# Scores of two key heads alternated in halves of the TensorE rows, with a new order of the attention steps

## The chip, the cores and the metric

The kernel runs on one core of one Trainium2 chip. The metric is the device time of one execution in microseconds (us). Engines are PE (TensorE, matrix products), DVE (VectorE), ACT (ScalarE), POOL (GpSimd) and SP (SyncE, which issues the transfers).

## What is computed

One inference step of a hybrid backbone of two layers, on 640 tokens of width 1024: 128 context tokens and 512 latent ones. A layer is an FFN, a mixer and a second FFN, each behind a modulated norm. The mixer has four parts of width 256, and this text is about three of them:

```python
IN_SPLITS = (H_A * HEAD_DIM, KV_A * HEAD_DIM, KV_A * HEAD_DIM, ...)     # H = 4 heads, KV = 2 key heads, HEAD_DIM = 64
def dense_attention(q, k, v, sink):                                      # B, and A's context tokens
    ...
    s = jnp.einsum('bqkgd,bskd->bkgqs', qi, k).astype(jnp.float32) * scale
    p = attn_probs(s, sink).astype(v.dtype)
    return jnp.einsum('bkgqs,bskd->bqkgd', p, v)
def window_attention(q, k, v, kc, vc, sink):                             # A: keys of +-128 tokens and 256 cached ones
    ...
    p = attn_probs(jnp.concatenate([s_ctx, s_band], axis=-1), sink).astype(v.dtype)
def retention_scan(q, k, v, log_g, S0):                                  # D, both directions
    ...
    inner = jnp.einsum('bhqd,bhsd->bhqs', qi, ki) * decay_mask
```

A is attention 0 (windowed, with a sink logit in the softmax), B attention 1 (dense). Both have four query heads in two groups g of two, one for each of the two key heads kv. The queries and keys are normed by head, scaled by a gain and turned by a rotary table. Part C is a recurrent branch.

## The kernel before, in words

Operands are float32, and a product is made of three products of their high and low parts, hi by hi, hi by lo, lo by hi (`mm3`, lines 271 to 275). ACT makes the high part of a weight (L168, whi or wp) and DVE the low part (L169, wlo).

Attention is worked in 20 items for each of A and B: five blocks b of 128 query tokens (the context, then four latent ones), two groups g, two key heads kv. A head has 64 channels, so the operands of the scores fill 64 of PE's 128 rows: kv 0 the upper half, kv 1 the lower. An item runs as follows. `scores`: PE makes the scores in a tile of two PSUM banks (sc): three products for the 256 cached keys, three for the tokens' own keys; in A one or two products with a mask (L1257) follow, on all 128 rows. DVE takes the maximum (mx, L1264) and its negative multiple (nm, L1268 or L1270); ACT takes the exponential of the scores and its sum (P, L1273), in A that of the sink (esink, L1276); DVE adds (L1277), inverts (rc, L1279) and scales (P, L1280). `trans`: PE transposes P in tiles of 128 columns (pt, L1290) and ACT copies (PT, L1291). `pv`, for both kv together: PE multiplies with the values (ao, L1299), ACT and DVE make the two parts (mxh, L1303; mxl, L1304).

The other work of the same stretch: `qkv`, the projections of queries, keys and values (nat, L1025 to L1027), with ACT's copies and squares (q, qsq), DVE's sum (qss, L1178, L1179), POOL's inverse root (qrr, L1181), DVE's product (q, L1183), POOL's gain (q, L1185), DVE's sine part (r, L1197), POOL's cosine part (q, L1200), DVE's addition (q, L1201); then transposes (tr, L1159) into the parts qkh and qkl (L1160, L1161). And `down`: output products of parts C and D (dn, twelve a call here), which DVE adds to the residual (x, L682).

`retention` makes scores in `scores` (rs, L1063, through `mm3`): for each of four key chunks j and two calls c, three products of 512 columns for one head, then three for the other.

What sets the order: the steps are Python generators, and the string ORDER has one letter for each step taken: m and M are scores and the rest of attention 0, n and N those of attention 1, p and q the two `qkv`, t and u their transposes, c the output products. "|" sets PSUM to two tiles of two banks (name S: the scores) and four of one bank (name M: nat, tr, pt, ao, dn). A scheduler with its own model then orders the instructions of each engine; each engine executes its own queue.

## Time and profile before

| | us |
|---|---|
| three runs | 2519.9, 2520.45, 2527.45 |
| median | 2520.45 |
| span of the profiled execution | 2521.9 |

The profile is of one execution, so rows are read against 2521.9 and compared with the median. Busy shares are of the whole span; the change touches the mixers only, and of these the retention (near 595 us in layer 0) and the attention (about 657 to 808 us in layer 0, 1896 to 2047 us in layer 1). A row of the timeline gives start, duration, engine, line, tiles written and read, and in brackets the time that the engine was idle before it and what ended that.

### The profile page before, as it was taken

To read this page: it belongs to the slowest core of one execution; us is meant where nothing else is said; L and a number is where in the kernel's file an instruction comes from. 1 tells how busy PE (TensorE), PEld (TensorE's weight loads), DVE (VectorE), ACT (ScalarE), POOL (GpSimd) and SP (SyncE) were. 2 spreads that over 40 slices of the span, in tenths; PEclk is the share of its full clock that TensorE was granted. 3 is DMA by queue.
4 is the path that set the end of the run, shared out by engine and by line. 5 is a ranking of instruction groups with operands and counts; after the bars stand their busy time and mean duration, and the time that the engine had idled before them with its cause. 6 is when DMAs were issued, how large, how long until landed. Compare 5 with 4: busy or idle time off the path is not lost.

```text
span 2521.9 us, 43865 instructions
## 1 busy us (share of the span) xinstructions
PE 2467.4 (98%) x17376; PEld 2365.6 (94%) x17376; DVE 1974.8 (78%) x3850; ACT 1141.8 (45%) x2271; POOL 244.8 (10%) x251
## 2 busy tenths in 40 slices
PE   7999999999999999999999999999999999999999
PEld 6999999996888999999999999999878789999999
DVE  6899989856666898988989898897656668666765
ACT  5344334563345633443463344344634556433433
POOL 2100000022420200000020000000433102000000
PEclk9999999999999999999999999999999999999999
DMA  7544344222102244443424444342110022222222
GB/s 253 185 152 138 127 129 148 94 78 67 37 18 66 93 144 134 143 133 118 141 89 148 134 142 133 119 134 78 58 60 26 18 76 76 77 67 81 87 81 71
DMA packets 92303, 261.88 MB, mean 104 GB/s; under 512 B 10049, under 2 KB 20929, under 8 KB 92097
## 3 DMA queue, kind: packets, MB, share of 16 engines
q1 hardware_dynamic: 92096, 259.07, 31.7%
q8 instruction: 137, 2.24, 0.4%
q14 instruction: 70, 0.57, 0.1%
HBM read 255.63 MB, written 3.41 MB: 103 GB/s over the span
## 4 chain that ended last, share of the span: by engine, by line
PE 67%; DVE 4%; ACT 2%; POOL 1%; issue 1%; DVEq 0%; POOLq 0%; ACTq 0%
PE dn L273 8%; PE dn L274 7%; PE dn L275 7%; PE x L274 5%; PE x L275 5%; PE x L273 5%; PE y L274 3%; PE y L275 3%; PE y L273 3%; PE pt L1290 2%; PE ao L1299 2%; PE g L274 2%; PE g L273 2%; PE g L275 1%; PE z L273 1%; PE z L274 1%
## 5 line engine op out<-in xcount | busy, mean ns | idle before, releaser
L273 PE MATMUL dn<-hidh,wp 128*128 128x320 f32 x1408 | 434.5, 311 | 0.0
L275 PE MATMUL dn<-hidh,wp 128*128 128x320 f32 x1408 | 433.9, 309 | 0.0
L274 PE MATMUL dn<-hidl,wp 128*128 128x320 f32 x1408 | 433.7, 309 | 0.2 <-DVE hidl L281 0.2
L168 ACT ACTIVATE wp<-ws 128x512 fp32r<-128x512 f32 x288 | 180.8, 630 | 393.2 <-DVE ws L215 149.9
L168 ACT ACTIVATE wp<-raw 128x512 fp32r<-128x512 f32 (+1 forms) x408 | 243.7, 611 | 212.1 <-DVE wp L169 84.2
L682 DVE SCALAR_TENSOR_TENSOR x<-dn,mod,x 128x128 f32<-128x128 f32 (+3 forms) x488 | 233.8, 518 | 126.4 <-PE dn L275 125.3
L318 DVE SCALAR_TENSOR_TENSOR junk<-wm,cond 128x1024 bf16<-128x1024 f32 x256 | 304.5, 1218 | 4.6 <-DMA wm<-in_wmod 4.5
L169 DVE TENSOR_TENSOR wp<-raw,wp 128x512 fp32r<-128x512 f32 (+1 forms) x408 | 266.2, 667 | 51.9 <-ACT wp L168 47.0
L273 PEld LDWEIGHTS dn<-hidh,wp 128*128 128x128 f32 x1408 | 264.5, 188 | 4.8 <-ACT hidh L280 3.7
L274 PEld LDWEIGHTS dn<-hidl,wp 128*128 128x128 f32 x1408 | 264.8, 188 | 0.6 <-DVE hidl L281 0.6
L275 PEld LDWEIGHTS dn<-hidh,wp 128*128 128x128 f32 x1408 | 264.6, 188 | 0.0
L169 DVE TENSOR_TENSOR wp<-ws,wp 128x512 fp32r<-128x512 f32 x288 | 197.4, 691 | 17.6 <-ACT wp L168 17.0
L274 PE MATMUL g<-hl,whi 128*128 128x320 f32 x608 | 192.6, 318 | 3.2 <-DVE hl L528 1.7
L275 PE MATMUL g<-hh,wlo 128*128 128x320 f32 x608 | 190.5, 314 | 0.0
L273 PE MATMUL g<-hh,whi 128*128 128x320 f32 x608 | 185.5, 318 | 4.5 <-ACT hh L527 2.2
L273 PE MATMUL x<-hh,wp 128*128 128x320 f32 x576 | 178.3, 310 | 1.0 <-DVE sl L613 1.0
L274 PE MATMUL x<-hl,wp 128*128 128x320 f32 x576 | 178.5, 310 | 0.0
L275 PE MATMUL x<-hh,wp 128*128 128x320 f32 x576 | 178.3, 309 | 0.0
L169 DVE TENSOR_TENSOR wlo<-raw,whi 128x1024 fp32r<-128x1024 f32 x88 | 109.8, 1249 | 61.2 <-ACT whi L168 46.0
L425 POOL TENSOR_TENSOR nrs<-nrm,neghalf 80x4 f32<-80x4 f32 x12 | 13.3, 1106 | 1377.1 <-DVE nrm L423 1377.1
L168 ACT ACTIVATE whi<-raw 128x1024 fp32r<-128x1024 f32 x88 | 92.5, 1052 | 80.5 <-PE dk L274 20.7
L274 PEld LDWEIGHTS g<-hl,whi 128*128 128x128 f32 x608 | 117.1, 193 | 5.9 <-DVE hl L454 3.5
(331 smaller groups left out, 6655.2 us busy)
## 6 DMA issues: line engine op xcount, KB each, us to landing
raw<-in_wgu SPq DMA_DIRECT2D x176, 512.0 KB, 3.5
wm<-in_wmod SPq DMA_DIRECT2D x128, 512.0 KB, 4.0
raw<-in_wd SPq DMA_DIRECT2D x64, 512.0 KB, 3.8
raw<-in_wd SPq DMA_DIRECT2D x32, 384.0 KB, 3.4
raw<-in_wint SPq DMA_DIRECT2D x20, 512.0 KB, 3.5
wm<-in_wm SPq DMA_DIRECT2D x32, 256.0 KB, 5.5
raw<-in_wqkv SPq DMA_DIRECT2D x16, 512.0 KB, 3.5
raw<-in_wocd SPq DMA_DIRECT2D x8, 512.0 KB, 3.4
```

Source lines behind the costliest of these rows:

```text
L168: S.activation(hi, src, AF.Copy)
L169: V.tensor_sub(lo, src, hi.bitcast(F32))
L273: PE.matmul(out, wh, xh, start=first, stop=False, skip_group_check=more)
L274: PE.matmul(out, wh, xl, start=False, stop=False, skip_group_check=more)
L275: mark["pe"] = PE.matmul(out, wl, xh, start=False, stop=last, skip_group_check=more)
L318: V.scalar_tensor_tensor(junk, modraw["w"], 1.0, cond[c], OP.mult, OP.mult, accum_out=modraw[(l, g)][:, c, k:k + 1])
L425: G.tensor_tensor(r, s, neghalf[:80, :4], op=OP.pow)
L682: V.scalar_tensor_tensor(x[d][:, s0:s1], pv[:, s0 - base:s1 - base], gate[:, c, d:d + 1], x[d][:, s0:s1], OP.mult, OP.add)
L1290: PE.transpose(p[:, c0 - a0:c0 - a0 + 128], P[:, c0:c0 + 128], idn)
L1299: PE.matmul(o[kv * 64:kv * 64 + 64, :128], vs[i][:, kv * 64:kv * 64 + 64], pts[kv][:, i * 128:i * 128 + 128], start=i == 0, stop=i == nb - 1)
```

## The change

`mm3s` issues the three products of two halves in turn: first product of A, first of B, second of A, and so on. The retention's scores use it. The items of an attention are now pairs (b, g): one step takes both S tiles, issues the scores of both key heads in turn, masks after them, and makes both softmaxes; one step of the rest transposes both and makes the products with v of the pair before. So m and n have 10 letters each in ORDER, and M and N 11, where they had 20 and 21. The part of ORDER from "|" on is new; the products are the same in number. Lines move by some: mx is L1268 after, nm L1271 or L1273, the exponential L1276, pt L1293, ao L1302, x L690.

```diff
+ROWS = (slice(0, 64), slice(64, 128))
 ORDER = (
-    "CaCCCCvLvrLarvvvLLLbsLvpLrprbrssrqsrsrLsptrsLpppqLp|!sputpLsptcqpcmccpMmqMmmcqtMmMmmqmMMmmqMqMcmcqMm"
-    "MuqmmqqccMMMmmmucMmMnnnuNcNNnnNnMNnnMNNmMncNncnnNNcnnNnNmnNNNMnNnNNnMccnMNNN",) * L
+    "CaCCCCvLvrLarvvvLLLbsLvpLrprbrssrqsrsrLsptrsLpppqLp|!sputpLsptcqpcmcmcpMtmqMmqMmqcMumqqMmqMmuqMmqMmq"
+    "cMuMncMnNncNncNncNncNncNncNnNncNcNcN",) * L
...
+        def mm3s(outs, whs, wls, xhs, xls, last=True):
+            n = range(len(outs))
+            for ws, xs, f, e in ((whs, xhs, True, False), (whs, xls, False, False), (wls, xhs, False, last)):
+                for i in n:
+                    PE.matmul(outs[i], ws[i], xs[i], start=f, stop=e)
...
                 def scores(j):
                     p = psS("rs")
-                    for hh in range(2):
-                        r0 = slice(hh * 64, hh * 64 + 64)
-                        ks = slice(128 + j * 128, 256 + j * 128)
-                        mm3(p[:, hh * 512:hh * 512 + 512], kh[r0, ks], kl[r0, ks], qh[r0, 128:640], ql[r0, 128:640],
-                            True, True)
+                    ks = slice(128 + j * 128, 256 + j * 128)
+                    mm3s([p[:, :512], p[:, 512:]], *([t[r, c] for r in ROWS] for t, c in (
+                        (kh, ks), (kl, ks), (qh, slice(128, 640)), (ql, slice(128, 640)))))
...
-                items = []
-                for b in range(5):
-                    for g in range(2):
-                        for kv in range(2):
-                            items.append((b, g, kv))
-                def scores(b, g, kv):
-                    p = psS("sc")
...
-                        mm3(p[:, 256:512], qh, ql, ckh[r, m * 256:m * 256 + 256], ckl[r, m * 256:m * 256 + 256], True, True)
-                        mm3(p[:, 512:512 + w], qh, ql, qkh[2][r, k0:k0 + w], qkl[2][r, k0:k0 + w], True, not band)
-                        for e, (j, i) in enumerate(band):
+                items = [(b, g) for b in range(5) for g in range(2)]
+                def scores(b, g):
+                    ps = [psS("sc") for _ in ROWS]
...
+                        mm3s([p[:, 256:512] for p in ps], *qs, *keys(ckh, ckl, slice(m * 256, m * 256 + 256)))
+                        mm3s([p[:, 512:512 + w] for p in ps], *qs, *keys(qkh[2], qkl[2], slice(k0, k0 + w)), not band)
+                        for p in ps:
+                            for e, (j, i) in enumerate(band):
...
+                    return [softmax(p[:, lo:hi], hi - lo, l * 4 + g * 2 + kv) for kv, p in enumerate(ps)], hi - lo, vs
...
-                    for b, g, kv in items:
-                        P, w, vs = q.pop(0)
-                        pts[kv] = trans(P, w)
+                    for b, g in items:
+                        Ps, w, vs = q.pop(0)
+                        pts = [trans(P, w) for P in Ps]
                         if ready:
                             pv(*ready)
-                        if kv == 1:
-                            ready = (b, g, (pts[0], pts[1]), vs)
-                            pts = {}
+                        ready = (b, g, pts, vs)
```

What the engines' queues look like at three places of layer 0 (numbers behind a name are those of the tile). PE at the start of the attention, before:

```order
L275 MATMUL dn_7147<-mxh_6985,wlo_6843 128x320
L273 MATMUL sc_7166<-qkh_6288,qkh_6286 128x128
L274 MATMUL sc_7166<-qkl_6291,qkh_6286 128x128
L275 MATMUL sc_7166<-qkh_6288,qkl_6289 128x128
L273 MATMUL dn_7183<-mxh_6567,whi_6842 128x320
```

One item, and behind it two calls of twelve dn and 24 of nat. PE after, first the pair and then what follows its twelve dn:

```order
L283 MATMUL sc_7166<-qkh_6288,qkh_6286 128x128
L283 MATMUL sc_7167<-qkh_6288,qkh_6286 128x128
L283 MATMUL sc_7166<-qkl_6291,qkh_6286 128x128
L283 MATMUL sc_7167<-qkl_6291,qkh_6286 128x128
L283 MATMUL sc_7166<-qkh_6288,qkl_6289 128x128
L283 MATMUL sc_7167<-qkh_6288,qkl_6289 128x128
L274 MATMUL dn_7200<-mxh_6567,whi_6842 128x320
```

```order
L276 MATMUL dn_7200<-mxh_6985,wlo_6843 128x320
L283 MATMUL sc_7214<-qkh_6288,qkh_6287 128x128
L283 MATMUL sc_7214<-qkl_6291,qkh_6287 128x128
L283 MATMUL sc_7214<-qkh_6288,qkl_6290 128x128
L274 MATMUL dn_7248<-mxh_6567,whi_6842 128x320
```

The first half of the second pair (sc_7214, in the place of sc_7166) now stands twelve dn behind the first pair. DVE at the same place, before:

```order
L1197 TENSOR_TENSOR r_7142<-q_7132,rsin_1362 128x8x16 x2
L1264 TENSOR_REDUCE mx_7170<-sc_7166 128x1
L1268 TENSOR_SCALAR nm_7172<-mx_7170,negsink_1376 128x1
L1201 TENSOR_TENSOR q_7132<-q_7132,r_7142 128x256
L1277 TENSOR_TENSOR sum_7175<-sum_7175,esink_7177 128x1
```

and after:

```order
L1200 TENSOR_TENSOR r_7142<-q_7132,rsin_1362 128x8x16 x2
L1268 TENSOR_REDUCE mx_7174<-sc_7166 128x1
L1268 TENSOR_REDUCE mx_7187<-sc_7167 128x1
L1204 TENSOR_TENSOR q_7132<-q_7132,r_7142 128x256
L1271 TENSOR_SCALAR nm_7176<-mx_7174,negsink_1376 128x1
L1271 TENSOR_SCALAR nm_7189<-mx_7187,negsink_1376 128x1
```

The two maxima stand together, and the addition of q stands ahead of nm, where it stood behind it. The second place is PE at the seventh windowed pair, before (scores of one item, transposes of q, then a projection):

```order
L273 MATMUL sc_7900<-qkh_6288,qkh_6286 128x384
L274 MATMUL sc_7900<-qkl_6291,qkh_6286 128x384
L1159 MATMUL tr_7852<-idn_96,q_7090 128x128
L1159 MATMUL tr_7852<-idn_96,q_7300 128x128
L1159 MATMUL tr_7852<-idn_96,q_7400 128x128
L1159 MATMUL tr_7852<-idn_96,q_7532 128x128
L1025 MATMUL nat_7859<-whi_7046,hh_5335 128x256
```

and after:

```order
L1259 MATMUL sc_7908<-masks_1364,idb_1366 128x128
L1162 MATMUL tr_7951<-idn_96,q_7748 128x128
L1162 MATMUL tr_7955<-idn_96,q_7748 128x128
L283 MATMUL sc_8033<-ckh_6854,qkh_6286 128x256
L283 MATMUL sc_8033<-ckl_6855,qkh_6286 128x256
L283 MATMUL sc_8033<-ckh_6854,qkl_6289 128x256
```

with DVE beside it:

```order
L1186 TENSOR_TENSOR q_7859<-q_7859,qrr_7865 128x256
L1200 TENSOR_TENSOR r_7869<-q_7859,rsin_1362 128x8x16 x2
L1204 TENSOR_TENSOR q_7859<-q_7859,r_7869 128x256
L1307 TENSOR_TENSOR mxl_7163<-ao_7894,mxh_7162 128x128
L1268 TENSOR_REDUCE mx_7925<-sc_7907 128x1
L1268 TENSOR_REDUCE mx_7938<-sc_7908 128x1
L1271 TENSOR_SCALAR nm_7927<-mx_7925,negsink_1376 128x1
```

Two transposes stand between the masks of a pair and the scores of the next (sc_8033, in the place of sc_7907), and the maxima of the pair before stand behind the rotary chain of q. The third place is ACT in the dense part, before:

```order
L1273 ACTIVATE P_8751,sum_8752<-sc_8740,nm_8749 128x768
L1291 ACTIVATE PT_8757<-pt_8758 128x384
L1291 ACTIVATE PT_8757<-pt_8763 128x384
L1303 ACTIVATE mxh_8265<-ao_8768 128x128
L1273 ACTIVATE P_8794,sum_8795<-sc_8783,nm_8792 128x768
L1291 ACTIVATE PT_8800<-pt_8801 128x384
```

and after:

```order
L1276 ACTIVATE P_8667,sum_8668<-sc_8649,nm_8665 128x768
L1276 ACTIVATE P_8677,sum_8678<-sc_8650,nm_8675 128x768
L1294 ACTIVATE PT_8697<-pt_8698 128x384
L1294 ACTIVATE PT_8697<-pt_8703 128x384
L1294 ACTIVATE PT_8708<-pt_8709 128x384
L1294 ACTIVATE PT_8708<-pt_8714 128x384
```

Exponentials and copies now come as two and four.

## Rows read from the trace of the kernel before

**Rows 1.** The page: busy time of each engine, and the chain that ended last.
```profile
PE 2467.4 (98%) x17376; PEld 2365.6 (94%) x17376; DVE 1974.8 (78%) x3850; ACT 1141.8 (45%) x2271; POOL 244.8 (10%) x251
...
PE 67%; DVE 4%; ACT 2%; POOL 1%; issue 1%; DVEq 0%; POOLq 0%; ACTq 0%
```
**Rows 2.** Stretches of 20 us: length, busy us by engine, granted clock, DMA share, GB/s.
```profile
720.00:740.00 20.00, 17.24 (x122) 14.41 (x120) 12.56 (x36) 8.06 (x22) 5.63 (x5) 0.83 0.04 16
...
760.00:780.00 20.00, 20.00 (x166) 16.43 (x162) 13.83 (x33) 11.12 (x27) 0.00 (x0) 1.00 0.08 27
```
**Rows 3.** Waits of PE, 640 to 820: total us, times, longest; two largest of five.
```profile
PE ao L1299 <- DVE x L682: 2.5, 1, 2.5
PE pt L1290 <- DVE P L1280: 1.7, 2, 1.5
```
**Rows 4.** Stretches of 2 us, columns as in Rows 2.
```profile
668.00:670.00 2.00, 0.55 (x7) 0.46 (x7) 1.93 (x7) 0.80 (x4) 0.72 (x1) 1.00 0.00 0
...
672.00:674.00 2.00, 2.00 (x11) 2.00 (x10) 1.65 (x11) 1.59 (x4) 0.46 (x1) 0.50 0.00 0
```
**Rows 5.** Instructions on the tile of the scores: busy us by engine (first PE).
```profile
640.00:820.00 180.00, 45.11 (x240) 28.77 (x216) 29.55 (x40) 32.74 (x80) 0.97 0.12 38
```
**Rows 6.** Timeline of PE in the dense part: start, us, engine, line, tiles.
```profile
765.06 0.38 PE L273 MATMUL sc<-ckh,qkh 64*128 64x256 f32 x1
...
766.31 0.42 PE L273 MATMUL dn<-mxh,whi 128*128 128x320 f32 x1
...
768.26 0.38 PE L273 MATMUL sc<-ckh,qkh 64*128 64x256 f32 x1
...
768.72 0.39 PE L273 MATMUL sc<-qkh 64*128 64x512 f32 x1
...
769.96 0.87 PE L1290 MATMUL pt<-idn,P 128*128 128x128 f32 x6
770.76 0.66 PE L1299 MATMUL ao<-PT,cv 128*64 128x128 f32 x8
...
772.22 0.55 PE L1290 MATMUL pt<-idn,P 128*128 128x128 f32 x3
772.70 0.38 PE L273 MATMUL sc<-ckh,qkh 64*128 64x256 f32 x1
```
**Rows 7.** Timeline of PE, then of DVE, at the first scores.
```profile
656.84 0.33 PE L273 MATMUL sc<-qkh 64*128 64x128 f32 x1
...
657.32 0.41 PE L273 MATMUL dn<-mxh,whi 128*128 128x320 f32 x1
...
661.65 0.28 DVE L1264 TENSOR_REDUCE mx<-sc 128x1 f32<-128x128 f32 x1
...
662.65 0.43 DVE L1201 TENSOR_TENSOR q<-q,r 128x256 f32<-128x256 f32 x1 [0.46 <-POOL q L1200]
```
**Rows 8.** Timeline of PE at the scores of the retention.
```profile
595.92 0.51 PE L273 MATMUL rs<-dqh,dkh 64*128 64x512 f32 x2
...
596.81 1.08 PE L1073 MATMUL ro<-pm,dvn 128*64 128x512 f32 x4
```
**Rows 9.** Timeline of DVE, then of ACT, after the two items of Rows 6.
```profile
769.61 1.82 DVE L1264 TENSOR_REDUCE mx<-sc 128x1 f32<-128x768 f32 x2
...
772.48 0.89 ACT L1273 ACTIVATE P<-sc,nm 128x768 f32<-128x768 f32 x1
...
773.35 0.86 ACT L1291 ACTIVATE PT<-pt 128x384 f32<-128x384 f32 x2
```
**Rows 10.** The chain that ended last, 705 to 730: start, us, what.
```profile
711.24 0.82 DVE mx L1264
712.06 0.33 DVE qss L1178
...
716.68 0.43 DVE q L1201
```
**Rows 11.** Groups of instructions by shape, 640 to 820: busy us, mean ns.
```profile
L1273 ACT ACTIVATE P<-sc,nm 128x640 f32<-128x640 f32 x8 | 6.4, 796 | 4.9 <-DVE nm L1268 2.6 <-DVE qss L1179 1.5 <-DVE rc L1279 0.8
```

More of the change, by code (lines that the diff above doesn't have):

```diff
@@ L1084, in retention @@
                 p = psS("rsc")
-                for hh in range(2):
-                    r0 = slice(hh * 64, hh * 64 + 64)
-                    mm3(p[:, hh * 512:hh * 512 + 128], kh[r0, 0:128], kl[r0, 0:128], qh[r0, 0:128], ql[r0, 0:128],
-                        True, True)
+                mm3s([p[:, :128], p[:, 512:640]], *([t[r, :128] for r in ROWS] for t in (kh, kl, qh, ql)))
                 pmc = thin("pmc", 256)
@@ L1231, in attention @@
                         mixed[2 * m + g] = (slot("mxh", F32R, T), slot("mxl", F32R, T))
-                items = []
-                for b in range(5):
-                    for g in range(2):
-                        for kv in range(2):
-                            items.append((b, g, kv))
-                def scores(b, g, kv):
-                    r = slice(kv * 64, kv * 64 + 64)
-                    qh, ql = qkh[g][r, b * 128:b * 128 + 128], qkl[g][r, b * 128:b * 128 + 128]
-                    p = psS("sc")
+                items = [(b, g) for b in range(5) for g in range(2)]
+                def scores(b, g):
+                    t0 = b * 128
+                    qs = [[t[r, t0:t0 + 128] for r in ROWS] for t in (qkh[g], qkl[g])]
+                    keys = lambda th, tl, c: [[t[r, c] for r in ROWS] for t in (th, tl)]
+                    ps = [psS("sc") for _ in ROWS]
                     if b == 0:
-                        mm3(p[:, 512:640], qh, ql, qkh[2][r, 0:128], qkl[2][r, 0:128], True, True)
+                        mm3s([p[:, 512:640] for p in ps], *qs, *keys(qkh[2], qkl[2], slice(0, 128)))
                         lo, hi = 512, 640
@@ L1253, in scores @@
                         band = [(j, i) for j, i in band if n0 <= j < n1]
-                        mm3(p[:, 512:512 + w], qh, ql, qkh[2][r, k0:k0 + w], qkl[2][r, k0:k0 + w], True, not band)
-                        for e, (j, i) in enumerate(band):
-                            c0 = 512 + (j - n0) * 128
-                            PE.matmul(p[:, c0:c0 + 128], idb, masks[:, i * 128:i * 128 + 128], start=False,
-                                      stop=e == len(band) - 1)
+                        mm3s([p[:, 256:512] for p in ps], *qs, *keys(ckh, ckl, slice(m * 256, m * 256 + 256)))
+                        mm3s([p[:, 512:512 + w] for p in ps], *qs, *keys(qkh[2], qkl[2], slice(k0, k0 + w)), not band)
+                        for p in ps:
+                            for e, (j, i) in enumerate(band):
+                                c0 = 512 + (j - n0) * 128
+                                PE.matmul(p[:, c0:c0 + 128], idb, masks[:, i * 128:i * 128 + 128], start=False,
+                                          stop=e == len(band) - 1)
                         lo, hi = 256, 512 + w
@@ L1261, in scores, with softmax @@
                         vs += [vn[:, 128 + j * 128:256 + j * 128] for j in range(n0, n1)]
-                    w = hi - lo
+                    return [softmax(p[:, lo:hi], hi - lo, l * 4 + g * 2 + kv) for kv, p in enumerate(ps)], hi - lo, vs
+                def softmax(p, w, si):
                     mx = small("mx", 1)
-                    V.tensor_reduce(mx, p[:, lo:hi], AX, OP.max)
+                    V.tensor_reduce(mx, p, AX, OP.max)
                     nm = small("nm", 1)
                     if m == 0:
-                        si = l * 4 + g * 2 + kv
                         V.tensor_scalar(nm, mx, -0.125, negsink[:, si:si + 1], OP.mult, OP.min)
@@ L1272, in scores @@
                     sums = small("sum", 1)
-                    S.activation(P[:, :w], p[:, lo:hi], AF.Exp, bias=nm, scale=0.125, accum_out=sums)
+                    S.activation(P[:, :w], p, AF.Exp, bias=nm, scale=0.125, accum_out=sums)
                     if m == 0:
@@ L1280, in scores @@
                     V.tensor_scalar(P[:, :w], P[:, :w], rc, None, OP.mult)
-                    return P, w, vs
+                    return P
                 def trans(P, w):
@@ L1313, in behind @@
                 def behind():
-                    pts = {}
                     ready = None
-                    for b, g, kv in items:
-                        P, w, vs = q.pop(0)
-                        pts[kv] = trans(P, w)
+                    for b, g in items:
+                        Ps, w, vs = q.pop(0)
+                        pts = [trans(P, w) for P in Ps]
                         if ready:
                             pv(*ready)
-                            ready = None
-                        if kv == 1:
-                            ready = (b, g, (pts[0], pts[1]), vs)
-                            pts = {}
+                        ready = (b, g, pts, vs)
                         yield
```

## The prediction, made before the changed kernel was run

> **What bounds the kernel now.** I read the page first: PE is busy for 98% of the span, DVE for 78%, ACT for 45%, and in the chain that ended last PE has 67% and DVE 4% [rows 1]. So an edit pays if it shortens the queue of PE, and costs if it makes PE wait. The mean hides the one place where PE does wait, so I then took stretches of 20 us across the attention of layer 0 (about 657 to 808.5 us; layer 1 has the same work at 1896 to 2047). In most of them PE is full, as in 760 to 780. Between 720 and 740 it is busy for 17.24 us only, at a granted clock of 0.83 [rows 2]. The waits of PE itself say for whom: 2.5 us for an evacuation on DVE and 1.7 us for a softmax on DVE are the two largest of five that sum to 6.0 us [rows 3]. One row more belongs to this: PE has 0.55 us of work in 668 to 670, and in 672 to 674 it runs at a granted clock of 0.50 (1.2 in place of 2.4 GHz) [rows 4]. An idle of some 1.5 us was followed by about 3 us at half clock. The baseline that follows: attention is a stretch in which PE is nearly the bound, with DVE 63 to 69% busy, so that what stands in which order on DVE matters.
>
> **The change part by part.**
>
> *Scores of one pair.* In 656.8 to 803 us the tile of the scores has PE for 45.11 us [rows 5]; counted from the start of each item to the start of what follows, item by item down the timeline, that is 41 us, since tails lie under the next instruction. One dense item alone, at 765.06, holds PE until 766.31: 1.25 us for its six products. Two that stand behind one another, at 768.26, are through at 769.96: 1.70 us, and the second starts at 768.72 beside the fourth product of the first [rows 6]. So halves of the rows do run at the same time where they are neighbours, and alternated they should take what one takes, 1.25 us. I take the same for the rest by their columns: 0.48 us for a pair of the context (one alone: 656.84 to 657.32 [rows 7]), 1.0 to 1.3 for a pair of the window, plus its masks, which use all rows and so do not pair. In the new order of instructions two context pairs alternate and two are split; of the eight windowed pairs five alternate, most with a transpose in between, and three stand as six of A, a mask, six of B, a mask; the eight dense pairs are between 1.25 and 1.7. That is 3 + 14 + 12, about 30 us a layer in place of 41: **11 us saved a layer, 22 in all**. Bounds: were all twenty pairs clean, some 21 us would do (20 saved a layer); if the split pairs gain nothing, 7 saved.
>
> *Scores of the retention.* Nothing. In the trace of before the two halves are issued as three and three, and yet each product of the one half has that of the other beside it (x2), and all six, 512 columns wide, lie between 595.92 and 596.81 [rows 8]: 0.89 us, what one half alone would take. I allow 0.1 us either way in each of the 20 groups, 2 us. The Trainium skill ("TensorE: Matmul & The Clock Gate", Part 3) says that matrix products start and end strictly in the order of the queue. By that rule all three of one half would have started before the other half's first, which with starts some 0.23 us apart is about 0.3 us more than the 0.89 seen, and the edit would bring 5 us over 16 groups; the trace does not agree.
>
> *New order: waits that it puts before PE.* The score tiles are two, and a pair takes both. Before, the next item could go into one tile while the other was being read; now the next pair starts only when the exponentials of the last have read their tiles. What that takes is in the trace, at a place where before too had two items together: scores end at 769.61, the two maxima run 1.82 us, the exponentials end at 772.48 and 773.35, and PE's next score starts at 772.70 in the first tile [rows 6, 9]. So a tile is back 3.1 us after its scores and the other one 3.9. That is free where PE has other work for 4 us. I walked along the new order of PE, DVE, ACT and POOL from the first score on with these durations, and PE has less than that at five places of a layer.
>
> (a) *The start.* Behind the first pair stand twelve products of the output (1.9 us), then the second pair's first half, which needs the first tile. Its exponential waits for nm (the negated maximum, the exponential's bias), which now stands on DVE behind both maxima and behind the rotary addition of q; that waits for POOL. In the trace the first maximum starts at 661.65 and that addition at 662.65, 0.43 long, whatever PE does [rows 7], since they hang on the chain of q. So nm ends at about 663.3, the exponential at 663.7. PE is through with the twelve at 656.8 + 0.5 + 1.9 = 659.2: **4.4 us idle**. Before, 24 products of the output and 24 of the projection stood there, and PE waited 0.2 us (the smaller of the two waits for P [rows 3]).
>
> (b), (e) *Two transposes of q* (the chunk of the latent tokens, then that of the second attention) stand where their chain ends about 2 us after PE arrives: **2 + 1.8**. The chain is 5 us long in the trace, from qss at 712.06 to the end of the addition at 717.1 [rows 10].
>
> (c) *Sixth windowed pair:* DVE has a weight's wlo (1.2 us) between the maxima of the fifth pair and nm; behind these come an exponential, mxh, esink and the second exponential (0.80 [rows 11]). From the scores' end 5.7 us; PE has 4: **1.8**.
>
> (d) *Seventh windowed pair:* only two transposes stand between the masks of the pair before and its own scores. The maximum of the pair before stands on DVE behind the whole chain of q (qss 712.06 to 717.1 in the analogous place [rows 10]). From the end of the projection: 1.2 us to qss, 5 of chain, two maxima of 0.82, nm and an exponential give 9.2; PE arrives after 4.7: **3 to 4.5**.
>
> (f), (g) *Dense part.* PE's work for a pair is 1.25 of scores, twice 0.80 of transposes, 1.46 of products with v and 1.95 of output products [rows 6], 6.3 us. ACT does both exponentials first and then the four copies of the transposes (the same shape as at 771.58 to 773.35, where a copy starts 2.6 us after its transposes ended [rows 9]); the products with v wait for the first copy, and the four small tiles of PSUM for the others. I get 6.9 us a pair: **4 a layer**, and 2 to 4 more where the dense part begins.
>
> Sum of new waits 18 to 22 us a layer; the 6 of before [rows 3] lie at places that the new order dissolves. Net +12 to +16 against -11: **+1 to +5 us a layer**. Half clock I enter at nothing net: before has it twice a layer [rows 2, 4], and after (a) and (d) it would come twice too. As a cross-check, my walk ends the dense part at about 812 where the trace has 808.5, +3.5.
>
> **Sum.** Two layers: +2 to +10, taken +6.5. The profiled execution, 2521.9 us, lies 1.45 above the median of the runs, 2520.45; the difference goes to the median: 2527. FFN, norms, loads and the order of the DMA queue are not touched.
>
> **Rivals.**
>
> *PE stays the bound (faster).* For it: PE is at 98%, the scores cost what they cost, and a walk with in-order queues tends to add up waits that the engines make good, because a PE that waits gives DVE time. If half of the new waits vanish, 2520 - 22 + 2 x 5 = 2508; if all beyond the old 6, 2498. Against it: (a) hangs on a time of DVE and POOL that PE cannot change. It would need (c), (d) and (g) all near zero.
>
> *The waits decide (slower).* One mechanism: score tiles come back late in the windowed part, where DVE carries both the chain of q and both maxima in one queue. At (a) and (d) PE idles 4 us and more, and the row at 672 says what follows, about 3 us at half clock [rows 4], or 1.6 us lost each. With (d) at its upper end, (c) twice and three half-clock stretches more than now, +9 a layer: 2539. It decides from 16 us of new net idle a layer. The Trainium skill states this cost: "TensorEngine Tiling (Array Packing)", PSUM Bottleneck, says that tiling speeds TensorE but not the evacuation of PSUM. Rows 9 agree with it: the tile's return took 3.1 to 3.9 us, longer than the 1.25 of its scores.
>
> *The change does nothing.* Halves overlap already in the retention [rows 8] and in part at 768.72 [rows 6]. If the queue of PE finds the second half by itself wherever it stands near, alternating saves only 0.4 us a pair, 8 us in 20 pairs of a layer at most, and if the waits are as few: 2520. Against it: items that stand alone, as at 765.06, do not overlap with anything.
>
> **How the numbers follow.** A measurement of this kernel can tell about 0.3%, 7.5 us. The forecast (waits give back the gain) has 0.50, between 2517 and 2537: 0.29 of it within 7.5 us, 0.21 above. PE-bound has 0.22, all faster. Waits decide 0.17, all slower. Does nothing 0.11, of which 0.10 within and 0.01 faster. So faster 0.23, same 0.39, slower 0.38. The range goes from 2500, where two thirds of the PE-bound case are in, to 2541; the forecast's own is 2517 to 2537.
>
> **What would show it.** Right: PE's busy time on the score tile falls by 10 us or more a layer; PE idle before the second pair is 4 us for an exponential on ACT; an idle of 3 us or more before the seventh windowed pair's scores; the spacing of dense pairs near 6.9 us; retention groups still near 0.89 us. Wrong: PE's idle in the attention stays near 6 us a layer (then faster), or the score time falls by less than 7 (then the pairs overlapped already), or the granted clock falls to half for more than 6 us a layer beyond now (then slower).

## The result and the profile after

The changed kernel takes 2562.37 us (median of four runs, 2553.38 to 2562.81) against 2521.34 us for the kernel before: a ratio of 1.0151, 95% interval 1.013 to 1.0171 (formed over all the runs, so not quite the quotient of the two medians). It is slower by 1.5%, 35 us above the forecast and 21 us above the upper end of the range. The profiled execution spans 2561.0 us, 39.1 more than the 2521.9 of before. Its page, section 1, busy us and share of each engine:

```profile
PE 2474.9 (97%) x17376; PEld 2372.2 (93%) x17376; DVE 1973.1 (77%) x3850; ACT 1140.8 (45%) x2271; POOL 242.9 (9%) x251
```

Shares of the whole span hide it again: PE has the same instructions, is busy 7.5 us longer, and the span is 39 longer. So I cut the program at the first score and at the first product of the next FFN (tile g) of each layer. One stretch is one row: bounds, length, busy us of PE, PEld, DVE, ACT and POOL, then the granted clock, DMA share and GB/s. Before, layers 0 and 1:

```profile
656.84:840.37 183.53, 177.90 (x1400) 154.74 (x1399) 117.91 (x328) 93.05 (x245) 24.65 (x32) 0.97 0.13 41
...
1897.44:2077.87 180.43, 175.08 (x1399) 151.91 (x1398) 119.08 (x329) 90.74 (x243) 24.61 (x32) 0.99 0.12 39
```

After:

```profile
656.28:861.93 205.65, 185.01 (x1420) 160.54 (x1419) 121.69 (x332) 95.75 (x249) 23.81 (x32) 0.91 0.12 39
...
1916.20:2119.49 203.29, 181.53 (x1420) 157.37 (x1419) 122.35 (x333) 92.74 (x246) 23.82 (x32) 0.92 0.12 37
```

Three numbers come out of such a row. Length less PE's busy time is idle. The clock column says how much of the stretch ran at half clock (1.2 in place of 2.4 GHz). Cut into the pieces that show 0.50, it gives PE's busy time at half clock; half of that is lost. Busy time less the lost time is the work that PE did, in us at full clock. In layer 0 idle went from 5.6 to 20.6, busy time at half clock from 10.0 to 38.1 (so the loss from 5.0 to 19.1), work from 172.9 to 165.9. The stretch grew by 22.1: +15.0 of idle, +14.1 lost to the clock, -7.0 of work. Layer 1 grew by 22.9: +16.4, +12.2, -5.7. The rest of the program became 5.9 us shorter in all; part of that is a sum of the next norm that moved across the second cut (below). 22.1 + 22.9 - 5.9 = 39.1.

Where PE idles, from its waits in the stretch of layer 0 (engine, tile, line, what it waited for: us in total, times, longest), the first four of twelve:

```profile
PE sc L283 <- ACT P L1276: 7.5, 3, 4.4
PE tr L1162 <- DVE q L1204: 4.3, 2, 2.3
PE ao L1302 <- ACT PT L1294: 1.8, 3, 0.9
PE ao L1302 <- DVE x L690: 1.2, 1, 1.2
```

Before, the list has an evacuation on DVE and a softmax on DVE at its head [rows 3]. Now the scores wait for the exponentials that still read their tiles, 4.4 us at the longest, and transposes wait for the chain of q. And what stands behind each of these idles, as stretches of layer 0: the idle before the second pair, then five stretches of PE at work (columns as above):

```profile
658.80:663.10 4.30, 0.00 (x0) 0.00 (x0) 2.58 (x10) 0.45 (x3) 1.95 (x3) 1.00 0.01 2
663.10:673.40 10.30, 10.24 (x42) 9.79 (x42) 3.80 (x19) 2.23 (x11) 0.00 (x0) 0.50 0.00 0
680.20:687.00 6.80, 6.80 (x37) 5.58 (x36) 4.88 (x16) 3.58 (x14) 1.61 (x3) 0.50 0.00 0
724.60:731.40 6.80, 6.80 (x29) 6.10 (x30) 3.60 (x12) 1.89 (x7) 0.00 (x0) 0.50 0.00 0
755.30:762.10 6.80, 6.60 (x36) 5.41 (x35) 3.19 (x11) 3.18 (x11) 0.00 (x0) 0.50 0.00 0
861.10:867.90 6.80, 6.80 (x31) 6.80 (x30) 5.08 (x11) 4.45 (x8) 1.24 (x1) 0.50 0.22 72
```

In all five PE is full, or nearly, and the clock column says 0.50. They stand behind idles of 4.38, 2.03, 2.39 and 2.28 us and behind the pauses of the norm. Two shorter ones of 3.4 us, behind idles of 0.74 and 0.82 us, make seven; all but 0.8 us of the last lies in the next FFN, outside the stretch. Before, layer 0 had two, 671.3 to 674.7 and 725.9 to 732.8, and layer 1 one of 3.4 us.

The start of the attention, on PE, then on DVE and ACT (start, us, engine, line, tiles; in brackets the idle before and what ended it), answers to [rows 7]:

```profile
656.28 0.33 PE L283 MATMUL sc<-qkh 64*128 64x128 f32 x2
...
658.47 0.31 PE L276 MATMUL dn<-mxh,wlo 128*128 128x320 f32 x1
663.16 0.47 PE L283 MATMUL sc<-qkh 64*128 64x128 f32 x1 [4.38 <-ACT P L1276]
...
664.42 0.47 PE L275 MATMUL dn<-mxl,whi 128*128 128x320 f32 x1
```
```profile
661.08 0.48 DVE L1268 TENSOR_REDUCE mx<-sc 128x1 f32<-128x128 f32 x2
...
662.06 0.43 DVE L1204 TENSOR_TENSOR q<-q,r 128x256 f32<-128x256 f32 x1 [0.50 <-POOL q L1203]
662.40 0.33 DVE L1271 TENSOR_SCALAR nm<-mx,negsink 128x1 f32<-128x1 f32 x2
```
```profile
662.65 0.37 ACT L1276 ACTIVATE P<-sc,nm 128x128 f32<-128x128 f32 x1 [7.36 <-DVE nm L1271]
```

This is step (a) as foretold: nm behind q's addition, the exponential behind nm, PE behind the exponential. And the next rows show the price that was not entered: the same dn product takes 0.31 us ahead of the idle and 0.47 behind it.

The retention, as in [rows 8], is as it was: 0.88 us from the first product to the next work, against 0.89.

```profile
576.48 0.50 PE L283 MATMUL rs<-dqh,dkh 64*128 64x512 f32 x2
...
577.36 1.08 PE L1079 MATMUL ro<-pm,dvn 128*64 128x512 f32 x4
```

The end of the stretch holds something that no step of the prediction spoke of. The norm of the next FFN, before and then after:

```profile
835.17 1.81 PE L421 MATMUL nsum<-ones,sq 128*80 128x1 f32 x24
...
840.37 0.93 PE L273 MATMUL g<-hh,whi 128*128 128x320 f32 x3
```
```profile
852.85 1.81 PE L429 MATMUL nsum<-ones,sq 128*80 128x1 f32 x24
...
856.95 0.49 PE L442 MATMUL nbc<-idn,nrs 80*128 80x80 f32 x4 [0.87 <-POOL nrs L433]
...
860.08 1.98 PE L429 MATMUL nsum<-ones,sq 128*80 128x1 f32 x20 [1.05 <-ACT sq L416]
861.93 1.15 PE L274 MATMUL g<-hh,whi 128*128 128x320 f32 x3
```

From the first sum to the first product of the FFN it takes 9.08 us in place of 5.20 (layer 1: 10.0 in place of 5.2). The scheduler now puts the second group of sums (x20) ahead of g, where before it stood behind the first products of g; it waits for ACT, and the broadcast nbc for POOL. Half clock follows.

### The profile page after: what moved, and what is told of

Read it like the earlier page. It is cut to its first block, busy times and chain, and to the rows that moved or that the text cites. A ratio compares the mean times of both kernels' runs of the same rounds, so it can differ in the third digit from the quotient of the medians.

```text
span 2561.0 us, 43866 instructions
## 1 busy us (share of the span) xinstructions
PE 2474.9 (97%) x17376; PEld 2372.2 (93%) x17376; DVE 1973.1 (77%) x3850; ACT 1140.8 (45%) x2271; POOL 242.9 (9%) x251
## 5 line engine op out<-in xcount | busy, mean ns | idle before, releaser
L690 DVE SCALAR_TENSOR_TENSOR x<-dn,mod,x 128x128 f32<-128x128 f32 (+3 forms) x488 | 234.4, 519 | 137.1 <-PE dn L276 135.3
L170 DVE TENSOR_TENSOR wp<-ws,wp 128x512 fp32r<-128x512 f32 x288 | 197.9, 692 | 17.8 <-ACT wp L169 17.3
L276 PE MATMUL g<-hh,wlo 128*128 128x320 f32 x608 | 191.2, 315 | 0.0
L433 POOL TENSOR_TENSOR nrs<-nrm,neghalf 80x4 f32<-80x4 f32 x12 | 15.2, 1265 | 1362.6 <-DVE nrm L431 1362.5
L1033 PE MATMUL nat<-whi,hh 128*128 128x256 f32 x400 | 120.5, 301 | 1.6 <-DVE kd L1112 1.3
```

The costliest lines, as they stand in the source:

```text
L170: V.tensor_sub(lo, src, hi.bitcast(F32))
L276: mark["pe"] = PE.matmul(out, wl, xh, start=False, stop=last, skip_group_check=more)
L433: G.tensor_tensor(r, s, neghalf[:80, :4], op=OP.pow)
L690: V.scalar_tensor_tensor(x[d][:, s0:s1], pv[:, s0 - base:s1 - base], gate[:, c, d:d + 1], x[d][:, s0:s1], OP.mult, OP.add)
L1033: PE.matmul(p[:, :n], hh[:, t0:t0 + 128], wh[:, w0:w0 + n], start=k == 0, stop=False)
```

## Experiments

The theory after this reading: the new order makes PE idle about as foretold, and each idle is paid a second time, since PE runs at half clock for a while behind it. The rivals: the loss lies in the alternation itself, or in the new order rather than in the pairs, or the idle only shifts work that would have waited elsewhere. One table serves all runs. It is worked out from each profiled execution as above, in us (length / idle / PE busy at half clock / work of the attention stretch). The third is PE's busy time summed over the pieces at clock 0.50; (1 - clock) x length of a row gives half of it within 2 us, since PE also idles in some of them. The fillers add work of their own, and the stretch of old_order has 48 products less, which stand ahead of its first score. The ratio is to the kernel before on the same chip, which took between 2521.34 and 2527.63 us, so between rows the ratios compare better than the times.

| kernel | time, median | ratio to before | layer 0 | layer 1 |
|---|---|---|---|---|
| before | 2521.34 | 1 | 183.5 / 5.6 / 10.0 / 172.9 | 180.4 / 5.3 / 3.3 / 173.4 |
| changed | 2562.37 | 1.0151 | 205.7 / 20.6 / 38.1 / 165.9 | 203.3 / 21.8 / 27.7 / 167.7 |
| changed_again | 2558.02 | 1.0125 | 199.1 / 21.8 / 19.2 / 167.8 | 202.1 / 22.0 / 24.6 / 167.9 |
| fill_a | 2552.77 | 1.0113 | 200.0 / 17.3 / 23.2 / 171.1 | 199.3 / 18.6 / 17.0 / 172.2 |
| fill_three | 2555.59 | 1.0122 | 198.7 / 16.8 / 11.1 / 176.4 | 203.3 / 16.7 / 20.3 / 176.5 |
| seq_halves | 2554.61 | 1.0119 | 198.2 / 19.7 / 21.3 / 167.9 | 200.5 / 20.8 / 23.2 / 168.1 |
| ret_only | 2522.44 | 0.9992 | 181.8 / 5.4 / 6.8 / 173.0 | 186.3 / 5.0 / 17.0 / 172.8 |
| old_order | 2564.45 | 1.016 | 202.6 / 19.4 / 41.6 / 162.4 | 199.7 / 19.1 / 35.2 / 163.0 |
| order_a | 2551.38 | 1.0106 | 196.8 / 17.2 / 27.3 / 166.0 | 196.6 / 18.5 / 23.7 / 166.3 |
| order_b | 2537.28 | 1.0051 | 190.1 / 14.2 / 16.4 / 167.7 | 189.8 / 15.2 / 13.0 / 168.1 |
| order_c | 2527.02 | 1.001 | 186.5 / 12.7 / 13.6 / 167.1 | 186.2 / 12.2 / 13.6 / 167.2 |
| order_c_seq | 2530.38 | 1.0018 | 184.1 / 12.7 / 6.8 / 167.9 | 185.3 / 12.4 / 10.2 / 167.8 |
| order_d | 2543.71 | 1.0068 | 191.2 / 16.6 / 16.0 / 166.7 | 197.2 / 15.3 / 32.9 / 165.4 |
| order_e | 2592.29 | 1.0258 | 217.8 / 26.9 / 38.6 / 171.7 | 219.6 / 26.5 / 42.4 / 171.8 |

**Filling the first idle.** The changed kernel, with one call of output products made three times, so that 24 more of them stand in the gap before the second pair.

```diff
-                        gemm(pv, u, xl, a, b, off=off, nk=nk, base=base)
+                        for _ in range(3 if (d, a) == (1, 320) else 1): gemm(pv, u, xl, a, b, off=off, nk=nk, base=base)
```

> The changed kernel, and in each layer the twelve output products that stand between the first two pairs of the attention are made three times over (the first two sets are overwritten): 24 products more, 3.5 us of work in the place where PE idled 4.38 us in the changed kernel. Theory A (the time beyond the waits is work at half clock that follows them): the 10 us at half clock behind that place go, worth 5 us a layer, and the work costs nothing, since it lies in the idle; 8 to 12 us faster than the changed kernel, about 2552. Theory B (the waits alone set the end, the half clock lies where PE has slack): no faster than the changed kernel, 2561 to 2563.

Measured: 2552.77 us, 1.0113 (1.0093 to 1.0132), 9.6 less than the changed kernel, with 48 products more in the program. PE of fill_a at the gap, and the stretch that was the first at half clock:

```profile
660.77 0.33 PE L283 MATMUL sc<-qkh 64*128 64x128 f32 x1 [0.90 <-ACT P L1276]
...
661.50 0.31 PE L275 MATMUL dn<-mxl,whi 128*128 128x320 f32 x1
```
```profile
660.80:671.10 10.30, 9.40 (x70) 8.68 (x70) 5.38 (x24) 3.03 (x14) 1.74 (x2) 1.00 0.01 2
```

The idle is 0.90 in place of 4.38, the dn behind it takes 0.31 in place of 0.47, and the clock of the 10.3 us is 1.00 in place of 0.50. Since 3.5 us of filler took the place of 3.5 us of idle, what was saved is the clock. So this wait of PE brings half clock with it, and other work in its place removes the half clock and most of the wait. The length of the half clock is not one figure, though: with this same wait (4.35 to 4.39 us) it was 3.4 to 10.2 us in the two layers of the changed kernel, of changed_again and of seq_halves, and there were cases in which it began before the wait had ended (by 2.3 us in layer 0 of seq_halves). In the four layers of fill_a and fill_three there was none.

**The changed kernel once more.** No edit.

> The changed kernel once more, beside the two others. Theory A: its executions differ by the number of stretches at half clock behind the same idles, 2551 to 2563, and the idles of its profile are those of the first one to 0.1 us (4.38, 2.03, 2.39, 2.28).

Measured: 2558.02 us, 1.0125 (1.0105 to 1.0144). The first wait and its half clock in this run, PE:

```profile
663.26 0.45 PE L283 MATMUL sc<-qkh 64*128 64x128 f32 x1 [4.39 <-ACT P L1276]
```
```profile
663.30:666.70 3.40, 3.40 (x13) 3.28 (x14) 1.37 (x6) 0.57 (x3) 0.00 (x0) 0.50 0.00 0
```

The four idles stand where they stood, 4.39, 2.03, 2.23 and 2.29 us in layer 0 (the third 0.16 shorter, with a new one of 1.34 ahead of it), but the half clock is 19.2 us in place of 38.1. So the idle of an order repeats from run to run within some 1 us a layer, and the half clock behind it does not: for this kernel, differences under some 10 us between two orders can be the clock's alone. That bounds what fill_a shows by its time; the clock at the spot itself is the firmer reading.

**Is it the alternation?** The changed kernel, with each call's three products of the one half issued ahead of the three of the other.

```diff
-            n = range(len(outs))
-            for ws, xs, f, e in ((whs, xhs, True, False), (whs, xls, False, False), (wls, xhs, False, last)):
-                for i in n:
-                    PE.matmul(outs[i], ws[i], xs[i], start=f, stop=e)
+            for i in range(len(outs)):
+                mm3(outs[i], whs[i], wls[i], xhs[i], xls[i], True, last)
```

> The changed kernel with its new order and its pairs, but the three products of the one half are issued before those of the other, in the attention and in the retention. Theory A (alternating is what shortens the scores): the score work grows back by 6 to 8 us a layer, 12 to 16 us slower than the changed kernel where PE is the bound, less where the additional work lies in idle time; 2566 to 2578. Theory B (PE's queue finds the second half by itself, as in the retention of before): 2560 to 2565.

Measured: 2554.61 us, 1.0119 (1.0096 to 1.0142), below both cases. Its work differs from that of the changed kernel by +2.0 and +0.4 us, and from changed_again by +0.1 and +0.2 (these two, the same kernel, differ by 1.9 and 0.2 themselves); half clock is 21.3 and 23.2 us. PE in a dense pair of seq_halves:

```profile
781.98 0.39 PE L274 MATMUL sc<-ckh,qkh 64*128 64x256 f32 x2
...
782.90 0.40 PE L276 MATMUL sc<-qkh,qkl 64*128 64x512 f32 x2
```

Each row is the same product of both halves (x2), though the second of the two is issued three places behind the first: the halves run beside each other without the alternation, and the pair takes 1.25 us as it does alternated. One might think that the scheduler had put the halves in turn by itself. The starts in the trace speak against it: within such a row they lie 10 ns apart here (781.975 and 781.985), and 3 or 4 ns apart where the program alternates (786.146 and 786.150 in the changed kernel), which fits more products standing between the two. That the halves stand together is worth something; in which order they are issued is worth nothing that these runs can tell.

**The retention alone.** The kernel before, with `mm3s` used in the retention only (both calls of `mm3` there replaced as in the change).

> The kernel before with alternated halves in the scores of the retention alone. My step says nothing changes: 2519 to 2524, and a group of six products of 512 columns takes 0.89 us as before. A rule of strict order in PE's queue would give about 5 us less, 2516.

Measured: 2522.44 us, 0.9992 (0.998 to 1.0005), with 0.90 us a group (574.26 to 575.16) against 0.89 [rows 8]. As foretold, nothing. The two starts of a row are mostly 9 or 10 ns apart in the kernel before and 3 or 4 ns here, so the edit did change the queue.

**Is it the new order?** The changed kernel with the order of before, its single items drawn together into pairs.

```diff
-|!sputpLsptcqpcmcmcpMtmqMmqMmqcMumqqMmqMmuqMmqMmqcMuMncMnNncNncNncNncNncNncNnNncNcNcN
+|!sputpLsptcqpcccpmqMmcqtMmqmMmqqMccqmMuqmqqccMmucMmnucNnNnMnNMcNncnNcnNmnNNnNMccnMNN
```

> The changed kernel with pairs and alternated halves, but in the order of before as far as it fits: of every two letters m, n, M, N the second stays. Theory A (the new order makes the waits, not the pairs): fewer idles of 2 us or more, less half clock, 2505 to 2530. Theory B (a pair that takes both score tiles makes the waits in any order): 2545 to 2570.

Measured: 2564.45 us, 1.016 (1.014 to 1.0179). Layer 0 in one row (columns as above):

```profile
659.98:862.58 202.60, 183.22 (x1372) 156.85 (x1371) 118.04 (x321) 97.36 (x250) 20.91 (x27) 0.89 0.12 40
```

It idles 19.4 us and is at half clock for 41.6. The waits are others (5.7 us for softmaxes on DVE, 4.1 for evacuations, seven waits for a score tile), their sum is near that of the changed kernel. So it isn't this one string: pairs that take both score tiles wait in the old order too.

**Filling three idles.** The changed kernel with three fillers: that of fill_a, one more call of output products made twice, and the products with v of one windowed pair made four times.

```diff
-                        gemm(pv, u, xl, a, b, off=off, nk=nk, base=base)
+                        for _ in range({(1, 320): 3, (2, 0): 2}.get((d, a), 1)): gemm(pv, u, xl, a, b, off=off, nk=nk, base=base)
...
-                    for i in range(nb):
+                    for i in [i for _ in range(4 if (m, b, g) == (0, 2, 0) else 1) for i in range(nb)]:
```

> The changed kernel with work in three of its idles in each layer: the 24 products more of fill_a at the start, 30 small products of an attention block with v once more three times over (2 us) behind the sixth windowed pair, where PE idled 2.39 us, and 12 output products twice (1.8 us) ahead of the transposes of the second attention, where it idled 2.28 us. All are overwritten. Theory A (idles cost twice, by themselves and by half clock behind them): the half clock at these places goes too, 3.4 us a place and layer beyond fill_a; 2536 to 2546. Theory B (only the first idle, the longest, matters to the clock): as fill_a, 2550 to 2556.

Measured: 2555.59 us, 1.0122 (1.01 to 1.0144). That is in the range of the second case, but not for its reason: some of the idles stayed. Idle fell by 3.8 and 5.1 us a layer only, although 10.5 and 8.8 us of work came in. PE at the seventh windowed pair, in the changed kernel and then in fill_three:

```profile
721.51 0.40 PE L1259 MATMUL sc<-masks,idb 128*128 128x128 bf16 x4
721.74 0.40 PE L1162 MATMUL tr<-idn,q 128*128 128x128 f32 x2
724.54 0.58 PE L283 MATMUL sc<-ckh,qkh 64*128 64x256 f32 x1 [2.39 <-ACT P L1276]
```
```profile
717.12 0.40 PE L1259 MATMUL sc<-masks,idb 128*128 128x128 bf16 x4
717.36 0.39 PE L1162 MATMUL tr<-idn,q 128*128 128x128 f32 x2
720.16 0.38 PE L283 MATMUL sc<-ckh,qkh 64*128 64x256 f32 x1 [2.41 <-ACT P L1276]
```

The filler of 60 products with v lies at 713.20 to 716.57, ahead of the last scores of the pair before, and pushes these along, while the chain of q gains 3.3 us. From the masks' start to the next scores it is 3.03 us in the one and 3.04 in the other. The wait is therefore the turn-around of a score tile, counted from the scores of the pair before, and not the chain of q, as step (d) had it. The half clock did fall, to 11.1 and 20.3 us.

**Other orders.** If the idles are the cost, orders that put PE's other work (q, c) behind each pair should take it back. Five strings, in the order in which they were tried, from the fourteenth sign behind "|" on:

```diff
-changed  cmcmcpMtmqMmqMmqcMumqqMmqMmuqMmqMmqcMuMncMnNncNncNncNncNncNncNnNncNcNcN
+order_a  cmccpmMqMctmcmqMmqMumqqMmqMmuqMmqMmqcMuMncMnNncNncNncNncNncNncNnNncNcNN
+order_b  cmccpmMqMctmcmqMmqMumqqMmqMcmuqMmqMmqcMcuMncMnNncNncNncNncNnNnNnNncNcNN
+order_c  cmccpmMqMctmcmqMmqMumqqMmqMcmquMmqMmqcMcuMncMnNncNncNncNncNnNnNnNncNcNN
+order_d  cmccpmMqcMtmcmqMmqMumqqMmqMcmquMmqMmqcMcuMncMnNncNnNncNncNnNncNncNnNcNN
+order_e  cmccpmMqcMtmcmqMmqMumqqMmqMcmquMmqMmqcMcuMncMnNNncNncNncNncNnNnNnNncNcN
```

> The changed kernel with another order of the same steps: between the first two pairs stand 24 output products and 24 of a projection in place of twelve, and the transposes of the last chunk of q come one projection and twelve output products later. Theory A: the idles of 4.38 and 2.03 us go, and with them 10 and 6.8 us at half clock of a layer; 14 us less a layer, at best 2535, with new small waits 2540 to 2550. Theory B (pairs that take both tiles wait somewhere else by as much): 2555 to 2570.

> As order_a, and twelve output products more stand ahead of the seventh windowed pair and ahead of the transposes of the second attention, so that all four idles of 2 us and more of the changed kernel have work in them; the dense part has four sets of output products less to hide its waits. Theory A: 2515 to 2535, full-speed work as in the changed kernel, idle 8 to 12 us a layer, half clock lost under 6. Theory B: the waits move into the dense part, 2545 to 2565.

> As order_b, and a projection (24 products, 2.8 us) stands between the masks of the sixth windowed pair and the seventh pair's scores, where order_b idles 2.41 us a layer. Theory A: that idle and some 3.4 us at half clock go, 4 us a layer: 2528 to 2533. Theory B (the wait only moves on): 2535 to 2540.

Measured: 2551.38 us, 1.0106 (1.008 to 1.0132); 2537.28, 1.0051 (1.0033 to 1.0069); 2527.02 beside 2526.73 for before on the same chip, 1.001 (0.9999 to 1.0021). The first two lie between the two cases of their expectations, the third 1 us under its own. Layer 0 of the three, columns as above:

```profile
654.65:851.49 196.84, 179.69 (x1399) 155.46 (x1399) 117.65 (x327) 94.18 (x245) 23.13 (x32) 0.93 0.12 39
```
```profile
654.36:844.43 190.07, 175.90 (x1399) 152.05 (x1399) 116.88 (x327) 93.80 (x245) 23.17 (x32) 0.96 0.12 40
```
```profile
654.99:841.54 186.55, 173.87 (x1400) 150.66 (x1399) 116.80 (x327) 93.27 (x245) 23.15 (x32) 0.96 0.12 41
```

Length less busy falls from 17.2 over 14.2 to 12.7, the clock comes back to 0.96, and the work stays at 166 to 168. Time followed idle and clock, with the pairs, the alternation and the work unchanged, so the loss is no price of the pairs as such. Of the step from the changed kernel to order_a, 4 to 5 us a layer are the norm's, whose second sums stand behind the first g again, and by its ratio order_a can't be told from changed_again; order_b and order_c can. In order_c PE saves 5.8 and 6.2 us of work a layer and pays 7.1 and 6.9 of idle and 1.8 and 5.1 of clock, and the kernel is level with before. What it still waits for, in a dense pair, PE:

```profile
779.32 0.39 PE L283 MATMUL sc<-ckh,qkh 64*128 64x256 f32 x2
...
780.57 1.53 PE L1293 MATMUL pt<-idn,P 128*128 128x128 f32 x12
783.69 0.38 PE L283 MATMUL sc<-ckh,qkh 64*128 64x256 f32 x1 [1.60 <-ACT P L1276]
```

The pair runs in 1.25 us, as the prediction took it from one item of before [rows 6]. The next scores come 3.1 us after its end, the time in which [rows 6, 9] gave a tile back; twelve transposes cover half of that. "TensorEngine Tiling (Array Packing)", PSUM Bottleneck, of the Trainium skill says so in words (tiling speeds up TensorE, not the emptying of PSUM), and this row agrees.

> As order_c, but the three products of one half are issued before those of the other. It parts what alternating itself brings from what standing together brings, in an order with little half clock. Theory A (PE takes up the second half by itself where both tiles are free): full-speed work 0.5 to 2 us a layer more than order_c, time within 4 us of it. Theory B (alternating brings the gain): 5 to 7 us of work a layer more, 10 us or more slower than order_c.

Measured (order_c with the edit of seq_halves): 2530.38 us, 1.0018 (1.0006 to 1.003), 3.4 us above order_c on the same chip, work +0.8 and +0.6 a layer. The alternation is worth under 1 us of work a layer here, and 3.4 us in all by the medians.

> As order_c, but twelve output products stand ahead of the transposes of the second context pair, where order_c idles 1.95 us a layer, and in the dense part the sets of output products are spread over the pairs (order_c idles 1.6 us for a score tile where two pairs have none between them). Theory A: idle falls from 12.5 to about 9 us a layer, half clock behind the first of them goes; 2516 to 2524, at or a little under the kernel before. Theory B (the waits move on): 2524 to 2532.

Measured: 2543.71 us, 1.0068 (1.0052 to 1.0083), outside both cases. The order closes one wait and opens two: from the waits of PE in layer 0,

```profile
PE ao L1302 <- ACT PT L1294: 3.2, 2, 2.9
...
PE tr L1162 <- POOL q L1203: 2.3, 1, 2.3
```

In layer 1 it idles 15.3 us, 3.1 more than order_c, and is at half clock for 32.9 against 13.6.

> As order_d in the windowed part, but in the dense part the next pair's scores come one step earlier, ahead of the transposes and products with v of the pair before, with all sets of output products in the first and last pairs. A pair then has less work between its scores and the next pair's, so if the return of the score tiles (3.1 us for the first, 3.9 for the second) sets the pace, idles of 1 us and more appear in the dense part: 2530 to 2550. If it does not, as order_d.

Measured: 2592.29 us, 1.0258 (1.0245 to 1.0271): the direction as expected, the size beyond it. Here nothing stands between two dense pairs but their own scores, PE:

```profile
788.00 0.40 PE L283 MATMUL sc<-qkh,qkl 64*128 64x512 f32 x2
791.47 0.58 PE L283 MATMUL sc<-ckh,qkh 64*128 64x256 f32 x1 [3.08 <-ACT P L1276]
```

This is the turn-around bare, 3.1 us of idle, and again the product behind it takes 0.58 us in place of 0.39. Waits for score tiles sum to 12.8 us in layer 0, half clock to 38.6.

None of these kernels is faster than the one before by more than the interval.

## Why the forecast was too low

*What bounds the kernel.* Right: PE, and where it must wait. Idle and the half clock behind it decided every order tried.

*Scores, 11 us a layer.* Too large: the work of the stretch fell by 7.0 and 5.7 us, in order_c by 5.8 and 6.2, at or under the lower bound of 7. PE's busy time on the score tile in layer 0 went from 45.11 [rows 5] to 39.58 us (37.32 in order_c). That is 5.5 less, under the 7 that the prediction named as a sign of pairs that overlap already, though part of the 39.58 is at half clock. (In the changed kernel the stretch also holds the sums that moved ahead of g, some 1.5 us; without them it is 8.5 and 7.2.) The price of a clean pair was right, 1.25 us; which pairs come out clean was not. And the third rival, that halves overlap by themselves wherever they stand near, was right as a mechanism: seq_halves and order_c_seq put the alternation at 0.1 to 2.0 us a layer, about what the changed kernel differs from its repeat. Its time, 2520, also needed few waits, and these did not stay few.

*Retention, nothing.* Right, by ret_only and by 0.88 us a group.

*New waits, 18 to 22 us, net +12 to +16.* Right in sum, in part by luck: net idle +15.0 and +16.4, with 1.9 us of the norm in it that no step had, and without (c). (The terms as listed add up to 19.0 to 22.5.) By step: (a) 4.4 foretold, 4.38 measured, by the chain named; (b) 2 and 2.03; (e) 1.8 and 2.28; (d) 3 to 4.5 and 2.39, for another reason, as fill_three showed; (c) 1.8, where the largest wait near it is 0.74; dense pairs stand 6.9 us apart as foretold (scores at 790.67, 797.65 and 804.51). The idle of 656.28 to 768 sums to 14.0, that of 768 to 835 to 4.7, the norm to 1.9.

*Half clock, "at nothing net".* This is the step that failed. The prediction expected two stretches of about 3 us in place of two. There were seven in layer 0 and five in layer 1, with 38.1 and 27.7 us of PE's busy time in the stretch, and the loss was +14.1 and +12.2 us a layer, nearly as much as the idle itself (+4.6 and +10.6 in changed_again). Nor did before, as profiled, have it "twice a layer": the rows were of layer 0, and layer 1 had it once. Of the 33 us by which the profiled execution grew more than the forecast's 6.5, the clock is 26, the work not saved 9, the idle 3, and the rest of the program took 6 back. The size was to be had beforehand: [rows 2] give 0.83 for 720 to 740, and 0.17 x 20 us is 3.4 us lost, 6.8 us at half clock, behind the 2.5 us of idle in [rows 3]. The prediction priced a stretch by the other place [rows 4], where 1.5 us of idle was followed by about 3. Closer, in before, where that idle of 2.5 us ends at 724.76, inside the first row:

```profile
723.40:725.90 2.50, 1.14 (x20) 1.10 (x20) 1.70 (x7) 0.05 (x1) 1.01 (x1) 1.00 0.00 0
725.90:732.80 6.90, 6.62 (x40) 5.53 (x36) 2.95 (x7) 2.18 (x6) 2.30 (x2) 0.51 0.00 0
```

With 2 to 2.5 us idle priced at 6.8 us of half clock, (a), (b), (d) and (e) alone lose 4 x 3.4 = 13.6 us a layer, 8.6 more than the two stretches of before cost by [rows 2, 4] (3.4 and 1.6), or 17 for two layers: the forecast would have stood at about 2544, over the upper end of the range. The work saved, 4 to 5 us a layer less than foretold, gives most of the rest. The prediction had named this itself as a sign of being wrong: half clock for more than 6 us a layer beyond now.

*"FFN, norms ... not touched".* Wrong by a side effect: in the changed kernel the scheduler put the second sums ahead of g, 3.9 and 4.8 us more from the first sum to the FFN. Since order_a to order_d, with the same pairs, take 5.1 to 5.3 us there, it hangs on the order and not on the pairs; on which part of the order is not shown (old_order, which ends in NN as they do, takes 11.3 and 8.7).

*The rivals.* "The waits decide" was the right one, with the right multiplier (clock) and in part the right place: score tiles that come back late are 7.5 of the 20.6 us in layer 0, the chain of q is 4.3. Its time, 2539, was too low for the same reason: it allowed three more stretches of 3 us each, where five more came in layer 0 and four in layer 1, of 3.4 to 10.2 us. "PE stays the bound" fell at step (a), as its own argument against it said.

Open: why an idle of about 2 us is followed by 3.4 us at half clock in one execution and 6.8 in another, and 4.4 us by 3.4 to 10.2; how much of the spread of the changed kernel's runs (2553.38 to 2562.81) this makes; and why order_d in layer 1 is at half clock so long for 3.1 us more idle.

## What to carry to other kernels

An idle of PE inside a dense stretch is to be priced at its length plus a third to the same again (0.3 to 0.9 of the added idle in the four layers of the changed kernel and its repeat), read from the granted clock of the stretch behind the nearest idle of that size, before any gain in matmul time is set against it. Two products in the two halves of the rows run beside each other when they stand near in the queue, so bringing them together is the gain and alternating them adds little. A step that takes every buffer of its kind needs as much other work behind it as one buffer takes to come back, here 3 to 4 us.

## What the runs showed of the hardware that I had not expected

The time at half clock behind an idle can be longer than the idle: 10.2 us behind 4.38, 6.8 behind 2.03, 2.28 and 2.39 in layer 0 of the changed kernel. At 2.03 PE came back at full clock, with products of 0.28 us, and fell only 0.8 us later, while full:

```profile
679.40 0.44 PE L1162 MATMUL tr<-idn,q 128*128 128x128 f32 x2 [2.03 <-DVE q L1204]
...
679.91 0.28 PE L1034 MATMUL nat<-whi,hl 128*128 128x256 f32 x1
...
684.27 0.41 PE L1033 MATMUL nat<-whi,hh 128*128 128x256 f32 x1
```

So the slow products need not stand right behind the wait that goes with them. And the same order with nearly the same idles gave 38.1 us at half clock in layer 0 of one execution and 19.2 in another, 3.4 us in place of 10.2 behind the longest idle.

The second thing is that PE begins products of the second half of the rows ahead of earlier ones of the first: in seq_halves both first products start at 781.98, 10 ns apart, although two others of the first half are issued between them. The rule of strict order that the prediction weighed ("TensorE: Matmul & The Clock Gate", Part 3, of the Trainium skill) does not hold for two halves of the rows here.
